# A transformer layer whose output projection goes from plain products to seven products per 2x2 split

## The chip, the cores and the metric

The kernel runs on one core of a Trainium2 chip. The engines named here are PE (TensorE, matmuls), DVE (VectorE), ACT (ScalarE), POOL (GpSimd) and SP (SyncE, which issues the DMA transfers). Each engine takes its instructions in the order of its own list and waits on semaphores for the others. The metric is the device time of one execution in microseconds (us).

## The reference, cut to what matters

One layer over 1024 tokens of width 1024: neighbourhood attention and retention, both from one input projection, merged by sigmoid gates, an output projection with a gated residual, a norm, and a gated convolutional MLP with a hidden width of 2816 (twice 22 blocks of 128).

```python
def _merge(o_na, o_ret, gate_na, gate_ret, w_proj_na, w_proj_ret, w_out):
    merged = jax.nn.sigmoid(gate_na) * (o_na @ w_proj_na) + jax.nn.sigmoid(gate_ret) * (o_ret @ w_proj_ret)
    return merged @ w_out
...
x = x + g1 * _merge(o_na, o_ret, xga, xgb, w_proj_na[l], w_proj_ret[l], w_out[l])
hx2 = _modulate(_rmsnorm(x, norm2_g[l]), sh2, sc2)
x = x + g2 * _conv_ffn(hx2, w_up[l], conv_w[l], conv_b[l], w_down[l])
...
def _conv_ffn(h, w_up, conv_w, conv_b, w_down):
    u = h @ w_up
...
    u = sum(up[:, i:i + n] * conv_w[i] for i in range(CONV_W)) + conv_b
    a, val = jnp.split(u, 2, axis=-1)
    return (jax.nn.silu(a) * val) @ w_down
```

## The kernel before, in words

Every float32 operand is split into a high and a low part in the matmul's own type (`split`: ACT casts the high part, DVE subtracts it to get the low one). A product is then three matmuls: high x high, high x low, low x high (`mm3`, `mm_a`, `open3`). A weight block reaches PE by `wload`: SP loads a raw tile of 128x512, ACT casts, DVE subtracts.

The stages, in order of time: input projection and neighbourhood attention (about 100 to 390 us of the span), retention (to 714), gates (768 to 921), the projection of the retention branch and the merge (`pret`, to 1008), output projection (to 1102), the MLP's up products (to 1540), the down projection (to 1752).

Large products are done in the manner of Strassen and Winograd: the two operands are cut in 2x2 and seven products of sums are made in place of eight. Class `Seven` does this for a unit of the gates and of the MLP's up product: it loads four weight blocks, POOL makes four sums s1 to s4 of them, and the steps 0 to 6 make the products A11 B11, S2 T2, S1 T1, S3 T3, A12 B21, A22 T4 and S4 B22. Here A stands for the weights and B for the activations; the T are differences of halves and quarters of the activations. The units are interleaved (`interleaved`), so that a unit's sums can be made in good time. The down projection uses the same seven products with the roles of the operands changed (table `DOWN`). Its weight sums are made beforehand: `down_sums` loads four blocks of w_down, has POOL subtract four times and stores the results in DRAM (`d_w`). Five of the eleven j are done in the retention, four in the gates (every third step), the last two beside `pret`.

In `pret` DVE multiplies a product by its gate, POOL adds the other branch, and the merged row block is split and kept (16 blocks, `mg`). The output projection is plain: `out_proj` makes, for each of 8 token blocks and 2 column halves, 8 x 3 matmuls. DVE multiplies by gate1 and adds x, ACT squares and sums, POOL takes the power, DVE scales: xn. `norm_out` transposes a token block (8 transposes of 128x128), ACT and DVE apply the modulation and split it, and for the second half of the tokens DVE makes the four T differences of that block and SP stores them to `d_t`. The MLP begins with two plain units (`up`, PLAIN = 2), in whose time `comb` loads and splits the T. `conv` follows each unit: ACT applies the middle tap from PSUM, DVE the two outer ones, ACT Silu, DVE the product; POOL makes sums for the down projection. From unit 2 on the units are `Up`, a `Seven`.

Order: the program's order is a start; when the kernel is built, a planner arranges each engine's list by estimated costs, SP's transfers among them. What is wrapped in `late` keeps its place in the program order on its engine. Pools of tiles with a fixed number of buffers set when a tile may be loaded again.

## Time and profile before

| | us |
|---|---|
| median of three runs | 1764.75 |
| the runs | 1764.75, 1764.78, 1760.84 |
| span of the profiled execution | 1759.2 |
| PE busy | 1726.0 (98%) |
| DVE busy | 1284.2 (73%) |
| ACT busy | 849.2 (48%) |
| POOL busy | 539.3 (31%) |

The profiled execution gives the span from its first to its last instruction; no run time of its own is listed beside it. In the views a stretch is given with its length, then for each engine its busy time and, in brackets, its number of instructions, and at the end PE's granted clock, the share of the DMA engines' time and GB/s. A group of instructions is given with line, engine, operation, output and inputs, its count, its busy time, the mean time of one in ns, and the idle time of the engine ahead of it with what ended that. A line of the timeline begins with the start and the duration in us; several instructions in a row are drawn together, with their count at the end. In a list of waits stand the total, the count and the longest.

### The profile page before, as it was taken

To read this page: it belongs to the slowest core of one execution; us is meant where nothing else is said; L and a number is where in the kernel's file an instruction comes from. 1 tells how busy PE (TensorE), PEld (TensorE's weight loads), DVE (VectorE), ACT (ScalarE), POOL (GpSimd) and SP (SyncE) were. 2 spreads that over 40 slices of the span, in tenths; PEclk is the share of its full clock that TensorE was granted. 3 is DMA by queue.
4 is the path that set the end of the run, shared out by engine and by line. 5 is a ranking of instruction groups with operands and counts; after the bars stand their busy time and mean duration, and the time that the engine had idled before them with its cause. 6 is when DMAs were issued, how large, how long until landed. Compare 5 with 4: busy or idle time off the path is not lost.

```text
span 1759.2 us, 24801 instructions
## 1 busy us (share of the span) xinstructions
PE 1726.0 (98%) x8405; PEld 1429.3 (81%) x8405; DVE 1284.2 (73%) x2454; ACT 849.2 (48%) x1826; POOL 539.3 (31%) x455
## 2 busy tenths in 40 slices
PE   8999999999999999999999999989999999999997
PEld 4688988888888888778888888778888888788886
DVE  4778887756776766777665557868899889875755
ACT  5666666653443434443444324534444444554444
POOL 1000000003334343555413300165555655211444
PEclk9999999999999999999999999999999999999999
DMA  9143334342231212677557733733322332586754
GB/s 348 61 130 125 95 117 147 117 133 87 73 108 43 72 42 68 203 238 239 200 199 268 246 143 132 254 108 102 108 90 92 118 120 90 170 296 192 239 162 162
DMA packets 139408, 261.10 MB, mean 148 GB/s; under 512 B 15856, under 2 KB 28304, under 8 KB 139280
## 3 DMA queue, kind: packets, MB, share of 16 engines
q1 hardware_dynamic: 139280, 259.51, 44.3%
q8 instruction: 66, 1.08, 0.3%
q14 instruction: 62, 0.51, 0.1%
HBM read 187.34 MB, written 69.48 MB: 146 GB/s over the span
## 4 chain that ended last, share of the span: by engine, by line
PE 43%; issue 6%; DVE 4%; POOL 3%; DMA 1%; ACT 1%; SPq 0%; POOLq 0%; ACTq 0%; DVEq 0%
PE u L1374 30%; PE y L1374 4%; PE pr L112 2%; PE pr L111 2%; PE pr L110 2%; PE om L122 1%; PE om L121 1%; PE om L123 1%; POOL x L1902 1%; DVE wc L87 0%; DVE b L1350 0%; DVE v L1679 0%; POOL pd L1939 0%; DVE hxT L87 0%; POOL x L1947 0%
## 5 line engine op out<-in xcount | busy, mean ns | idle before, releaser
L1374 PE MATMUL u<-T,wc 128*128 128x512 f32 x960 | 227.1, 392 | 5.1 <-ACT pu L1408 5.1
L1374 PEld LDWEIGHTS u<-T,wc 128*128 128x128 f32 x960 | 180.6, 189 | 45.7 <-ACT pu L1408 7.9
L1374 PE MATMUL y<-wc,ahl 128*128 128x512 f32 x924 | 210.6, 389 | 2.7 <-DVE wc L87 1.8
L1374 PEld LDWEIGHTS y<-wc,ahl 128*128 128x128 f32 x924 | 173.3, 188 | 39.7 <-DVE wc L87 2.5
L87 DVE TENSOR_TENSOR wc<-ur,wc 128x512 fp32r<-128x512 f32 x137 | 122.7, 897 | 65.8 <-ACT wc L86 65.8
L86 ACT CAST wc<-ur 128x512 fp32r<-128x512 f32 x137 | 85.0, 621 | 129.7 <-PE y L1374 72.3
L111 PE MATMUL mm<-low,wc 128*128 128x512 f32 (+1 forms) x328 | 124.0, 378 | 0.0
L1374 PE MATMUL u<-h2a,wc 128*128 128x512 f32 x480 | 112.3, 389 | 0.7 <-DVE pu L1417 0.7
L110 PE MATMUL mm<-hx,wc 128*128 128x512 f32 x264 | 107.4, 407 | 0.2 <-ACT wc L589 0.2
L1374 PEld LDWEIGHTS u<-h2a,wc 128*128 128x128 f32 x480 | 90.0, 188 | 19.8 <-DVE pu L1417 1.2
L112 PE MATMUL mm<-hx,wc 128*128 128x512 f32 x264 | 105.2, 399 | 0.0
L86 ACT CAST wc<-s 128x512 fp32r<-128x512 f32 x80 | 49.7, 623 | 93.2 <-PE u L1374 88.3
L123 PE MATMUL mm<-wc,low 128*128 128x512 f32 (+1 forms) x240 | 91.2, 380 | 0.0
L1374 PE MATMUL u<-hxT,wc 128*128 128x512 f32 x384 | 89.6, 389 | 0.0
L1508 POOL TENSOR_TENSOR col<-col,bcol 128x32 f32<-128x32 f32 x1 | 0.3, 253 | 280.7 <-DVE aw L538 280.7
L87 DVE TENSOR_TENSOR wc<-s,wc 128x512 fp32r<-128x512 f32 x80 | 83.5, 1046 | 3.8 <-ACT wc L86 3.4
L1374 PEld LDWEIGHTS u<-hxT,wc 128*128 128x128 f32 x384 | 72.1, 188 | 14.9
L87 DVE TENSOR_TENSOR wc<-raw,wc 128x512 fp32r<-128x512 f32 x92 | 68.0, 746 | 17.7 <-ACT wc L86 17.7
L121 PE MATMUL mm<-wc,hx 128*128 128x512 f32 x192 | 75.2, 392 | 0.6 <-ACT r L1105 0.6
L122 PE MATMUL mm<-wc,hx 128*128 128x512 f32 x192 | 75.2, 392 | 0.0
L1383 POOL TENSOR_TENSOR s<-ur 128x512 f32<-128x512 f32 x20 | 35.7, 1783 | 126.3 <-DVE wc L87 68.7
L86 ACT CAST wc<-raw 128x512 fp32r<-128x512 f32 x92 | 56.8, 621 | 33.0 <-PE pr L112 6.0
(393 smaller groups left out, 4671.3 us busy)
## 6 DMA issues: line engine op xcount, KB each, us to landing
ur<-in_w_up SPq DMA_DIRECT2D x80, 256.0 KB, 2.9
ur<-d_a SPq DMA_DIRECT2D x77, 256.0 KB, 3.1
aw<-in_w_ada SPq DMA_DIRECT2D x32, 512.0 KB, 3.3
pj<-in_w_down SPq DMA_DIRECT2D x44, 256.0 KB, 5.2
d_w<-pj SPq DMA_DIRECT2D x44, 256.0 KB, 2.0
d_a<-sa SPq DMA_DIRECT2D x44, 256.0 KB, 2.0
ur<-d_w SPq DMA_DIRECT2D x44, 256.0 KB, 3.8
d_a<-at SPq DMA_DIRECT2D x33, 256.0 KB, 2.7
```

The lines of the kernel that those rows point to most:

```text
L86: act.copy(hi, src)
L87: (lo_eng or vec).tensor_tensor(lo, src, hi.bitcast(F32), ALU.subtract)
L110: pe.matmul(out, wh, xh, start=k == 0, stop=False)
L111: pe.matmul(out, wh, xl, start=False, stop=False)
L112: pe.matmul(out, wl, xh, start=False, stop=k == n - 1)
L121: pe.matmul(out, ah, bh, start=first, stop=False)
L122: pe.matmul(out, ah, bl, start=False, stop=False)
L123: pe.matmul(out, al, bh, start=False, stop=last)
L1374: pe.matmul(out, a, b, start=first and n == 0, stop=last and n == 2, skip_group_check=True)
L1383: pool.tensor_tensor(self.s1, self.a21, self.a22, ALU.add)
L1508: pool.tensor_tensor(col[:, 16:48], col[:, 16:48], bcol[:, 16:48], ALU.add)
L1902: pool.tensor_tensor(z, z, fg[:, gs(dh)], ALU.mult)
```

## The change

- `out_sums` makes the four sums of w_out for each of four j during the attention: six loads of 256 KB (two blocks are loaded twice), four POOL subtractions and four stores to `d_wo`, with three buffers, driven by one `next(wsums)` per attention step. The sums of w_down that stood beside `pret` move to the gates, which now run them every second step.
- `pret` keeps the merged rows as they are, without splitting, in SBUF; `mg_sums` makes S1 to S4 of them on DVE.
- The output projection takes the seven products in the order of the down projection: for each product p and each j a pair of operands is loaded and split (`out_ops`), and four token blocks are multiplied (`out_steps`). Multiplication by gate1 and addition of x go to POOL (`gated`), but for the last product of each column half (`out_last`), with the small steps of the norm.
- The transposes go by k over four token blocks (`turn2`), mixed with the plain up products, which now run in four loops: unit 1 with half 1, unit 0 with half 1, unit 0 with half 0, unit 1 with half 0. POOL makes the T differences (`token_sums`).
- Units 2 and 3 make their two products without sums first (`head`: A11 B11 and A12 B21), ahead of the interleaved steps.
- The plain units' products are copied from PSUM by ACT before `conv`.

```diff
+    def out_sums():
+        def load(j, n):
+            t = na.tile([P, 512], F32, tag="os", bufs=3, name="os")
+            sync.dma_start(t, io["w_out"][n % 2, KH * (n // 2) + j])
+            return t
+
+        for j in range(KH):
+            b11, b12 = load(j, 0), load(j, 1)
+            yield
+            late(pool.tensor_tensor(b12, b12, b11, ALU.subtract))
+            b22 = load(j, 3)
+            yield
+            sync.dma_start(d_wo[j, 0], b12)
+            late(pool.tensor_tensor(b22, b22, b12, ALU.subtract))
...
+            sync.dma_start(d_wo[j, 2], y)
...
         if i == 0:
             ada_load()
+        if i > 2:
+            next(wsums, None)
...
-    RET_SUMS, GATE_SUMS = 5, 9
+    RET_SUMS = 5
...
-    gate_sums = down_sums(gr, RET_SUMS, GATE_SUMS)
+    gate_sums = down_sums(gr, RET_SUMS, NH)
...
-        if n % 3 == 1:
+        if n % 2:
             next(gate_sums, None)
...
+    ORDER = (("A11", "B11"), ("S2", "T2"), ("A12", "B21"), ("S3", "T3"), ("S1", "T1"), ("A22", "T4"), ("S4", "B22"))
...
-        h_, l_ = gtile(half, F32R, "mh"), gtile(half, F32R, "ml")
-        split(h_, l_, g)
-        mg[db, half] = (h_, l_)
...
+    def mg_sums(j):
+        for c, x, y, o, n in (("S1", "A21", "A22", ALU.add, 1), ("S2", "S1", "A11", ALU.subtract, 0), ("S3", "A11", "A21", ALU.subtract, 0), ("S4", "A12", "S2", ALU.subtract, 1)):
+            am[c, j] = gtile(n, F32, "s")
+            vec.tensor_tensor(am[c, j], am[x, j], am[y, j], o)
...
+    def out_ops(p, js):
+        tl = []
+        for j in js:
+            w = wload(out_source(j, ORDER[p][1]))
+            a = pair_tile("ahl")
+            split(a[:, 0], a[:, 1], am[ORDER[p][0], j])
+            tl.append((j, a, w))
+        return tl
...
+    def out_last(tb, dh, p, x):
+        z[tb, dh] = t = t_tile("z")
+        vec.tensor_tensor(t, bank(p % 2, tb % QB), gate1[:, cols(dh)], ALU.mult)
+        vec.tensor_tensor(t, t, x, ALU.add)
+        out_square(tb, dh)
+        s = ss[:, tb]
+        pool.tensor_scalar(s[:, 3:4], s[:, dh : dh + 1], 1.0 / D, s[:, 2:3], ALU.mult, ALU.add)
+        pool.tensor_tensor(s[:, 4:5], s[:, 3:4], mhalf[:, 0:1], ALU.pow)
...
+    def gated(t, tb, dh):
+        pool.tensor_tensor(t, t, gate1[:, cols(dh)], ALU.mult)
+        pool.tensor_tensor(t, t, x_rows(tb, dh), ALU.add)
...
+    def token_sums(k):
+        b11, b21, b12, b22 = v2[0, k], v2[0, k + KH], v2[1, k], v2[1, k + KH]
+        for c, o, x, y in ((0, b11, b12, b11), (2, b12, b22, b12), (1, b22, b22, b11), (3, b21, b21, b22)):
+            pool.tensor_tensor(o, x, y, ALU.subtract)
+            sync.dma_start(d_t[c, k], o)
...
+    out_steps(1, True, False)
+    for b in range(QB):
+        u2[b] = t_tile("u2")
+        vec.tensor_tensor(u2[b], bank(1, b), p1[b], ALU.add)
+    for b in range(QB):
+        gated(u2[b], b, 1)
...
+    for n in range(2):
+        for b in range(QB):
+            out_mm(6, b, t7[n : n + 1], False, True)
+    for b in range(QB):
+        turn2(1, KORD[b], bank(1, 2 + b % 2))
+        out_mm(6, b, t7[2:], False, True)
+        out_last(b, 1, 6, u2[b])
...
+    for n, k in enumerate(KORD):
+        turn2(0, k, bank(0, n % 2))
+        if k >= KH:
+            token_sums(k - KH)
+        for br in range(2):
+            up_k(us4[2 + br], wu[1][br], 1, k, n)
...
+        def head(self):
+            self.X, self.p1 = u_tile(), self.tmp()
+            self.prod(self.X, self.raw(self.src[0, 0]), "B11", True, False)
+            act.copy(self.p1, self.X)
+            self.prod(self.X, self.raw(self.src[0, 1]), "B21", False, True)
+            self.c11()
...
+    for n in range(PLAIN):
         for c in ((1, 0), (2, 3))[n]:
             combs[f"T{c + 1}"] = comb(c)
-        conv(j, *us2)
+        uu = [tap.tile([P, T], F32, tag="uu", bufs=4, name="uu") for _ in range(2)]
+        for br in range(2):
+            for half in range(2):
+                act.copy(uu[br][:, half * 512 : half * 512 + 512], us4[2 - 2 * n + br][half])
+        conv(seq[n], *uu)
     units = [Up(n, j) for n, j in enumerate(seq)]
+    for i in range(PLAIN, PLAIN + HEADS):
+        units[i].head()
     for i, n in interleaved(PLAIN, NF):
-        units[i].step(n)
+        if i >= PLAIN + HEADS or n not in (0, 4):
+            units[i].step(n)
```

More of the change, by code (lines that the diff above doesn't have):

```diff
@@ L1040, in tile_hybrid_layer @@
     for _ in pieces:
+        pass
+    for _ in wsums:
         pass
@@ L1617, in tile_hybrid_layer @@
             pret(db, half)
-            next(out_sums, None)
-    pjp.release()
-    wo = {}
-    for kb in range(KB):
-        t = wop.tile([P, 2, 512], F32R, tag="wo", bufs=KB, name="wo")
-        wo[kb, 0] = wload(io["w_out"][0, kb], into=t)
+        if db >= KH:
+            mg_sums(db - KH)
     hxpool.release()
@@ new lines, in out_mm, with out_steps, out_square @@
+    def out_mm(p, b, tl, first, last):
+        ts = slice(b * P, (b + 1) * P)
+        for j, a, w in tl:
+            open3(bank(p % 2, b), a[:, 0, ts], a[:, 1, ts], w[:, 0], w[:, 1], first and j == 0, last and j == KH - 1)
+    def out_steps(p, first, last, n=KH):
+        for j in range(n):
+            tl = out_ops(p, (j,))
+            for b in range(QB):
+                out_mm(p, b, tl, first, last)
+    z, xn, v2 = {}, {}, {}
+    def out_square(tb, dh):
+        junk = t_tile("junk")
+        act.activation(junk, z[tb, dh], AF.Square, accum_out=ss[:, tb, dh : dh + 1])
+        sync.dma_start(d_x1[tb * P : (tb + 1) * P, cols(dh)], z[tb, dh])
@@ new lines, in tile_hybrid_layer @@
+    out_steps(3, False, False)
+    for b in range(QB):
+        u3[b] = t_tile("u3")
+        vec.tensor_tensor(u3[b], bank(1, b), p1[b], ALU.add)
+    for b in range(QB):
+        gated(p1[b], QB + b, 0)
+    out_steps(4, True, False)
+    for b in range(QB):
+        z[QB + b, 1] = u3[b]
+        vec.tensor_tensor(u3[b], bank(0, b), u3[b], ALU.add)
+        gated(u3[b], QB + b, 1)
+        out_early(QB + b, 1)
+    out_steps(5, False, True, 2)
+    tl = out_ops(5, (2, 3))
+    t7 = out_ops(6, (0, 1))
@@ L1719, in tile_hybrid_layer @@
+    wu[0] = [up_load(seq[1], br) for br in range(2)]
+    for br in range(2):
+        for n in range(KB):
+            up_k(us4[br], wu[0][br], 0, n, n)
     op.release()
@@ L1780, in comb @@
     def comb(c):
-        t = [tpl.tile([P, 4, KH, P], F32R, name=f"T{c}{i}") for i in range(2)]
-        for b in range(4):
-            raw = ur_load(d_t[c, b])
-            split(t[0][:, b], t[1][:, b], raw.rearrange("p (k t) -> p k t", k=KH))
+        t = [tpl.tile([P, KH, 512], F32R, name=f"T{c}{i}") for i in range(2)]
+        for k in range(KH):
+            split(t[0][:, k], t[1][:, k], ur_load(d_t[c, k]))
         return t
@@ L1815, in dst @@
         def dst(self, b, half):
-            return self.u[b][:, half * 512 : half * 512 + 512]
+            return self.out(b)[:, half * 512 : half * 512 + 512]
         def c11(self):
```

246 lines of the change are left out of this document (127 added, 119 removed).

## The prediction

> **What bounds the kernel now.** I read the engines' shares first, then stretches of 44 us, then the waits of PE, SP's timeline, and the groups of POOL, DVE and ACT.
>
> ```profile
> span 1759.2 us, 24801 instructions
> PE 1726.0 (98%) x8405; PEld 1429.3 (81%) x8405; DVE 1284.2 (73%) x2454; ACT 849.2 (48%) x1826; POOL 539.3 (31%) x455
> ...
> PE u L1374 <- ACT pu L1408: 5.1, 1, 5.1
> ...
> 1052.00:1096.00 44.00, 44.00 (x211) 36.59 (x211) 30.77 (x82) 16.88 (x38) 2.19 (x4) 1.00 0.34 130
> 1140.00:1184.00 44.00, 38.85 (x165) 31.73 (x164) 30.61 (x36) 16.65 (x25) 30.14 (x18) 0.96 0.35 115
> 1188.00:1232.00 44.00, 44.00 (x195) 36.16 (x194) 39.44 (x41) 21.12 (x30) 22.21 (x13) 1.00 0.34 107
> ```
>
> PE is the bound nearly everywhere (98% busy; the third column of a stretch is its busy time). A full stretch holds 195 matmuls of 128x512, so one costs 44 / 195 = 0.2256 us; the longer time shown for a single one overlaps its neighbours. The stretch from 1052 holds 211, of which 32 are the 128x128 transposes L1671: (44 - 179 x 0.2256) / 32 = 0.113 us each. The one large hole inside is in the stretch from 1140: 30 matmuls are missing and the granted clock is 0.96. The wait behind it is the 5.1 us in PE's list. Hence two rules for what follows: a matmul removed is 0.2256 us won; and as PE has no slack after a wait, a new wait of PE is lost in full.
>
> The median of the runs is 1764.75 us, 5.5 us more than the profiled span. I take these 5.5 us as unchanged and apply the sum to both alike.
>
> **1. Fewer products.** Eight row blocks x 2 column halves x 8 k x 3 = 384 matmuls become 7 products x 4 blocks x 4 j x 3 = 336; transposes (64) and plain up products (192) keep their number. -48 x 0.2256 = **-10.8 us**.
>
> **2. The old wait before the first sum unit.** It is meant to be filled by the two heads (48 matmuls, 10.8 us).
>
> ```profile
> 1150.35 1.07 PE L1374 MATMUL u<-T,wc 128*128 128x512 f32 x4
> 1156.57 3.62 PE L1374 MATMUL u<-T,wc 128*128 128x512 f32 x8 [5.15 <-ACT pu L1408]
> ```
>
> PE stops at 1150.35 + 4 x 0.226 = 1151.3 and resumes at 1156.57: 5.3 us. The next eight take 3.62 us, where eight at full rate take 0.39 + 7 x 0.226 = 1.97: after a wait of this length about 1.65 us more go to the half-speed clock. Gone: **-6.9 us**. I add 1.7 us to each new wait of several us below.
>
> **3. Weight sums ahead of the attention.** In the changed program SP's list has, between the load of aw and the copy of kH0, ten loads of w_out, five stores to d_wo and the two raw loads that stood there before; each store waits for a POOL subtraction, and with three os buffers the fourth and later loads wait for a subtraction or for a store that has landed. SP takes its list in order, so kH0 waits behind all of them.
>
> ```profile
> 87.62 0.42 SPq L530 DMA_DIRECT2D aw<-in_w_ada  x1
> 93.08 4.94 SPq L91 DMA_DIRECT2D raw<-in_w_qkv  x2
> 98.15 1.17 SPq L409 DMA_DIRECT2D kH<-kH  x2
> ...
> raw<-in_w_qkv SPq DMA_DIRECT2D x1, 256.0 KB, 2.7
> ...
> kH<-kH SPq DMA_DIRECT2D x1, 320.0 KB, 4.1
> raw<-in_w_qkv SPq DMA_DIRECT2D x1, 256.0 KB, 3.2
> d_w<-pj SPq DMA_DIRECT2D x44, 256.0 KB, 2.0
> ...
> 102.28 0.39 PE L112 MATMUL mm<-hx,wc 128*128 128x512 f32 x1
> 102.51 0.28 PE L472 MATMUL sl<-kH,qS 128*128 128x256 f32 x1
> ...
> L1901 POOL TENSOR_SCALAR ssf<-ssf 128x1 f32<-128x1 f32 x8 | 3.2, 400 | 1.4 <-ACT xr L1897 0.8
> L1907 POOL TENSOR_TENSOR ssf<-ssf,mhalf 128x1 f32<-128x1 f32 x8 | 4.7, 586 | 0.5
> L1593 POOL TENSOR_TENSOR sg<-sg 128x512 f32<-128x512 f32 x14 | 19.9, 1421 | 86.9 <-DVE sg L1592 77.3 <-DMA raw<-in_w_pret 4.2 <-ACT wc L86 2.9
> L1939 POOL TENSOR_TENSOR pd<-pd,xr 128x512 f32<-128x512 f32 x4 | 6.8, 1740 | 0.0
> 1201.57 1.29 POOL L1384 TENSOR_TENSOR s<-s,ur 128x512 f32<-128x512 f32 x1 [3.14 <-issue]
> ```
>
> The copy starts at 98.15 and takes 4.1 us, so kH0 lands at 102.3 and PE, having issued its last product at 102.28, reads it at 102.51: no slack. The new list, with a load at 2.6, a subtraction at 1.3 (the solitary POOL row) plus 0.5 for its start, a store at 2.0, an issue at 0.4: loads from 88.0; first store issued 93.0 and landed 95.2; the second store 94.6; load of x 95.3; third store 98.0, landed 100.2; y loaded at 98.4, subtracted by 102.8; fourth store 103.0, landed 105.2; the next j's b12, asked for at 103.4, is subtracted by 107.8; its store 108.0; then a load, raw and kH0 at 109.2. That is 11.0 us after 98.15. PE's scores, in order, come 10.9 us later: with the clock **+12.6 us**. Bounds: 0 if the chain were run before 98; 18 if its loads take 3.2 and its subtractions 1.74 (L1939). I take the short times of the nearest rows, since little else is moving there. The later sums stand among the ada loads, and PE reads the next kH only after sixteen more score products: 0 (to 2).
>
> **4. Gates and pret.**
>
> ```profile
> L1249 POOL TENSOR_TENSOR pj<-pj 128x512 f32<-128x512 f32 x44 | 62.7, 1426 | 7.5 <-DMA pj<-in_w_down 7.0
> ```
>
> The subtractions for w_down in the gates rise from 16 to 24, 8 x 1.43 = 11 us more of POOL over some 150 us, with eight loads and stores more. In pret DVE gets 16 row sums and loses 16 splits of merged rows, ACT loses 16 casts. I allow **+1 us** (0 to 3) for one late sum.
>
> **5. The seven products.** S is their start; one lasts 48 x 0.2256 = 10.8 us. POOL now multiplies by gate1, adds x and makes the small ops of the norm, in this order: u2 8 ops, z 4 with a small one after each that waits for ACT's square, p1 8, u3 8 with 4 small, then two small ones for each out_last.
>
> ```profile
> 1201.96 1.45 DVE L87 TENSOR_TENSOR wc<-s,wc 128x512 fp32r<-128x512 f32 x1
> ...
> L1654 ACT ACTIVATE xn<-x 128x1024 f32<-128x1024 f32 x1 | 1.1, 1063 | 0.2 <-DVE x L1651 0.2
> L87 DVE TENSOR_TENSOR wc<-s,wc 128x512 fp32r<-128x512 f32 x20 | 19.9, 1002 | 3.5 <-ACT wc L86 3.4
> L87 DVE TENSOR_TENSOR wc<-raw,wc 128x512 fp32r<-128x512 f32 x6 | 4.1, 684 | 0.0
> ```
>
> A split that DVE begins at 1201.96, while POOL is busy from 1201.57 to 1202.86, takes 1.45 us where it takes 0.684 alone: it ends 0.55 after POOL's. So the two get in each other's way; here DVE makes two splits per step of 2.7 us beside POOL. POOL's price lies between 1.29 (alone) and 1.74 (L1939, with the same splits at the same pace); I take 1.6. u2 is there at S + 22.5: ends 35.3; z: 4 x (1.6 + 0.4 + 0.75 for a square of half L1654's size, an estimate from its 1.06 with the sum's read-out) = 11, 46.3; p1 12.8, 59.1; u3 12.8 + 1.6, 73.5; four pairs of 0.4 and 0.586, 77.4; scaling, 78. PE wants all four blocks of xn after product six and two steps of seven: 26 x 2.71 = S + 70.4. Wait 7.6, with the clock **+9.3 us**. Bounds: 1 at 1.29 (POOL then waits for product five), 13 at 1.74.
>
> On this the Trainium skill, "SBUF — State Buffer", section "SBUF: two separate sides", is stricter: a DVE operation with two SBUF inputs and a GpSimd operation that reads SBUF hold a shared pair of ports in turn, the other "fully blocks". The row agrees that the split waited; the pair above took 1.84 us where blocking alone would give 1.97. That every POOL op meets a split is the first rival.
>
> **6. Turns, plain ups, and the heads.** Loop 2 turns half 0 and has POOL make 16 token sums; loops 3 and 4 are products only. From its start L2, PE takes 32 x 0.113 + 144 x 0.2256 = 36.1 us to the end U of loop 4. In the changed program DVE's and ACT's lists after the turns are: T2, T1, conv of the first unit, T3, T4, conv of the second, and only then the heads' weights; the heads' banks also wait for ACT's copies of u. Before, conv read PSUM and the T were long there.
>
> ```profile
> d_t<-v SPq DMA_DIRECT2D x4, 256.0 KB, 2.0
> ur<-d_t SPq DMA_DIRECT2D x4, 256.0 KB, 3.2
> ...
> L86 ACT CAST T<-ur 128x512 fp32r<-128x512 f32 x16 | 8.9, 617 | 3.5 <-DMA d_t<-vo 3.3 <-DMA ur<-d_t 0.2
> L1762 ACT ACTIVATE ta<-ta 128x1024 f32<-128x1024 f32 x5 | 5.3, 1061 | 8.4 <-DVE ta L1761 8.4
> L1759 ACT ACTIVATE ta<-uu,cb,cw 128x1024 f32<-128x1024 f32 x3 | 3.7, 1245 | 1.7 <-DVE uu L1398 1.7
> L1408 ACT COPY pu<-u 128x512 f32<-128x512 f32 x5 | 2.9, 574 | 2.1 <-PE u L1374 2.1
> L1762 ACT ACT_TABLE_LOAD x1 | 1.3, 1283 | 0.0
> L87 DVE TENSOR_TENSOR T<-ur,T 128x512 fp32r<-128x512 f32 x16 | 10.2, 684 | 2.3 <-ACT T L86 2.3
> L1763 DVE TENSOR_TENSOR at<-ta,at 128x1024 f32<-128x1024 f32 x5 | 6.1, 1214 | 0.0
> L1760 DVE SCALAR_TENSOR_TENSOR ta<-uu,cw,ta 128x1023 f32<-128x1023 f32 x3 | 3.9, 1285 | 0.0
> ```
>
> POOL's first token sum can start after two turns of 1.8 us and DVE's pass, L2 + 5; six at 1.6 beside the turns, ten at 1.29: done at L2 + 27.5. SP issues the T loads behind all sixteen stores; the fourth goes out at 29.1 and lands 3.2 later: D = L2 + 32.3. From D, ACT: a cast, four T1 casts and four copies of u (4.8), ta (1.245): 6.7. DVE: four steps of conv, 5.1: 11.8; T3, 2.7: 14.5; its last sum, 1.2, after ACT's table load and Silu: 15.7; T4: 18.4. ACT meanwhile: at, T3, half T4 to 11.6, table and Silu to 14.0, rest of T4, four copies of u to 17.5, ta to 18.75. DVE's second conv 5.1: 23.9; the split of the first head weight 0.68: 24.6. The heads run from L2 + 56.9, PE is free at 36.1: 20.8, with the clock **+22.5 us**. Bounds: 16 with every token sum at 1.29, no table load and loops that DVE makes 3 us longer; 28 with every sum at 1.74. The heads are behind the very chain they should cover; what follows them is covered.
>
> In loop 1 DVE has four gate/add/scale groups beside four turns, but POOL's lateness in step 5 has let it catch up: 0 (to 3).
>
> **Sum.** -10.8 - 6.9 + 12.6 + 1 + 9.3 + 22.5 = +27.7: span 1786.9, time 1764.75 + 27.7 = **1792 us**.
>
> **Rivals.** (a) Full exclusion of POOL and DVE: each POOL op of step 5 costs 1.29 + 0.68 = 1.97 and xn is ready at S + 88: 17.6 + 1.7 instead of 9.3, and two more us on the token sums: 1804. For it: the split row; against: L1939's 1.74. Chance 0.12. (b) SP's chain is hidden, because the stores and loads of the sums overlap more than I let them: 1792 - 12.6 = 1779. For it: SP's raw load at 93.08 came 5 us after the ada load even without the sums. 0.12. (c) The chain from token sums to conv ends near U, the heads then do their work: 1792 - 22.5 = 1770. Against: 24.6 us of DVE and ACT work between D and the heads, each piece with its row. 0.1. (d) The other side: a waiting instruction doesn't hold what stands behind it. Then kH0 goes at 98, the heads' splits pass conv, and only steps 1, 2, 4 and 5 are left: 1764.75 - 17.7 + 1 + 9.3 = 1757, faster by 0.4%. It decides as soon as steps 3 and 6 together cost less than 7 us. Against it stand two rows:
>
> ```profile
> SPq L91 <- DVE wc L87: 14.9, 5, 5.0
> ...
> 1153.50 1.26 DVE L87 TENSOR_TENSOR wc<-ur,wc 128x512 fp32r<-128x512 f32 x1 [2.67 <-ACT wc L86]
> ```
>
> Between 84 and 106 us SP stands 14.9 us for raw buffers that DVE frees, and issues nothing meanwhile; in the old gap DVE stands 2.67 us for a cast. 0.1, a third of which ends as no change. That the heads simply don't fill the gap they are named for is my forecast, step 6.
>
> **Chances and range.** The forecast holds 0.56, with its own range 1784 to 1800. Going down to (c) and up to (a), 1769 to 1805 leaves out (d) and the far ends. About 0.3% (5 us) is what tells a change from none here. Faster 0.08, same 0.04, slower 0.88.
>
> **What would show it.** Step 1: 336 products in the out stage. Step 3: kH's copy issued near 109 instead of 98, PE idle some 11 us before its first scores. Step 5: PE waiting for xn before the first half-1 transposes, POOL ops of 1.5 to 1.75 us, no gap on POOL. Step 6: T's loads behind d_t's last store, PE idle some 20 us after the last plain up product, ended by a head's wc. Wrong would be: kH copied on time; POOL at 1.3 us; heads starting within 5 us of loop 4.

## The result, and the profile after

The changed kernel takes 1836.09 us (median of four runs, 1830.01 to 1839.51) against 1764.76 before: a ratio of 1.0401, 95% interval 1.0379 to 1.0424. The forecast was 1792 and its range ended at 1805. The direction came as forecast, the size did not: +71 us instead of +27.7.

The profiled execution took 1830.01 us, the fastest of the four, with a span of 1828.2; by spans the change costs 69.0 us. A run is thus some 1.8 us longer than its span. The 5.5 us that the prediction carried between span and median before were mostly the spread between runs, not a fixed cost.

First the head of the page of the kernel after, then its stretches of the output stage up to the first transpose of xn, of the rest up to the last plain up product, and of the 36 us behind that. The columns are those of the stretches shown before.

```profile
span 1828.2 us, 24941 instructions
PE 1736.2 (95%) x8357; PEld 1428.1 (78%) x8357; DVE 1322.5 (72%) x2378; ACT 860.8 (47%) x1842; POOL 635.7 (35%) x531
```

```profile
1028.84:1128.51 99.67, 78.72 (x314) 59.69 (x312) 68.19 (x82) 38.39 (x77) 46.43 (x40) 0.92 0.42 134
1128.51:1204.06 75.55, 65.27 (x280) 49.47 (x280) 50.16 (x68) 32.15 (x57) 28.93 (x28) 0.92 0.43 151
1204.06:1240.00 35.94, 18.40 (x60) 13.00 (x61) 33.73 (x27) 21.10 (x34) 22.37 (x12) 0.72 0.51 164
```

PE fell from 98% to 95% busy. In the first stretch no engine is full: PE 79 of 100 us, DVE 68, ACT 38, POOL 46. That is the picture of engines waiting for each other, not of one that has too much work. It is the main thing that the prediction missed: 312 products at 0.2256 us are 70.4 us, so 29.3 us are lost there.

Where the 69.0 us lie, by the start of each stage's first PE instruction in the two timelines:

| stage | before, us | after, us | difference | forecast |
|---|---|---|---|---|
| to the first scores | 102.5 | 115.1 | +12.6 | +10.9 (step 3) |
| attention | 300.2 | 305.0 | +4.8 | +1.7 (step 3, the slow clock behind the wait) |
| retention, transposes, gates | 518.1 | 519.2 | +1.1 | 0 |
| projection and merge | 87.0 | 89.5 | +2.4 | +1 (step 4) |
| output projection to the last plain up product | 140.0 | 175.2 | +35.3 | -1.5 (steps 1, 5, loop 1) |
| rest | 611.4 | 624.2 | +12.8 | +15.6 (steps 2, 6) |

**The start.** SP's timeline of the kernel after, and PE's wait there:

```profile
88.10 1.37 SPq L1011 DMA_DIRECT2D os<-in_w_out  x3
94.81 0.33 SPq L1020 DMA_DIRECT2D d_wo<-os  x1
...
110.29 1.17 SPq L409 DMA_DIRECT2D kH<-kH  x2
```

```profile
115.14 0.55 PE L472 MATMUL sl<-kH,qS 128*128 128x256 f32 x1 [10.99 <-DMA kH<-kH]
```

The copy of kH goes out at 110.29 (before: 98.15; forecast: 109.2), behind the stores to `d_wo`; PE stands 10.99 us, and the products after it run slow for a while (the next three start 0.35, 0.22 and 0.21 us apart, before 0.12).

**The seven products.** From the list of waits between 1028 and 1130 us, three of PE and two of ACT:

```profile
ACT wc L86 <- DMA raw<-d_wo: 25.3, 4, 11.0
...
ACT junk L1725 <- POOL u L1746: 10.0, 4, 3.8
...
PE u L1752 <- DVE z L1734: 7.6, 1, 7.6
PE u L1408 <- DVE ahl L87: 7.5, 5, 2.6
...
PE u L1408 <- ACT ahl L86: 5.6, 5, 2.0
```

Read from the bottom: PE waits ten times, 13.1 us together, for a split pair (`ahl`), and once, 7.6 us, ahead of the first transposes of xn. The other 8.6 of the 29.3 us lost are products at a slower pace (granted clock 0.92). ACT's casts of weights wait 25.3 us in four pieces for raw tiles. Why the tiles are late stands in SP's timeline:

```profile
1053.90 10.52 SPq L1688 DMA_DIRECT2D xr<-in_x  x4
1064.55 4.73 SPq L91 DMA_DIRECT2D raw<-d_wo  x4
...
1085.64 10.03 SPq L1688 DMA_DIRECT2D xr<-in_x  x4
...
1105.61 10.44 SPq L1726 DMA_DIRECT2D d_x<-u  x4
```

Three times SP needs 10 us for four transfers. The row tiles of x have four buffers, which come free with POOL's additions; the stores of x wait for those additions themselves. While POOL works through its eight operations, SP issues no weights. ACT has the same trouble: its squares (`junk`) wait 10.0 us for POOL, with casts behind them.

The groups of DVE and POOL from 1050 to 1122 us give the second part, and the timeline shows one burst:

```profile
L87 DVE TENSOR_TENSOR wc<-raw,wc 128x512 fp32r<-128x512 f32 x16 | 20.0, 1266 | 15.6 <-ACT wc L86 15.6
L1745 POOL TENSOR_TENSOR u<-u,gate 128x512 f32<-128x512 f32 x8 | 12.4, 1561 | 38.2 <-ACT wc L86 30.5 <-DVE u L1806 7.7
...
L87 DVE TENSOR_TENSOR ahl<-s,ahl 128x512 fp32r<-128x512 f32 x10 | 11.5, 1156 | 6.7 <-ACT ahl L86 6.7
...
L87 DVE TENSOR_TENSOR ahl<-sg,ahl 128x512 fp32r<-128x512 f32 x6 | 8.0, 1344 | 1.4 <-ACT ahl L86 1.4
```

```profile
1053.84 1.74 POOL L1745 TENSOR_TENSOR u<-u,gate 128x512 f32<-128x512 f32 x1
...
1054.35 1.78 DVE L87 TENSOR_TENSOR wc<-raw,wc 128x512 fp32r<-128x512 f32 x1
```

POOL's price, 1.49 to 1.59 us in the mean of a group, is close to the 1.6 that I took. But the price is paid by both: DVE's splits cost 1.16 to 1.34 us in the mean, up to twice the 0.684 of before, and in a burst the two engines go in step, some 1.7 us for a split beside a POOL operation.

The wait of 7.6 us is another matter. It is ended not by xn but by `z` L1734: the third block's product is read out of the PSUM bank that the first transposes are to write. On DVE this reading stands behind xn of the two blocks before it, and each xn waits for POOL's two small operations, which wait for ACT's square of that block. DVE's timeline, then POOL's:

```profile
1122.95 0.49 DVE L1741 TENSOR_SCALAR xn<-z,ss 128x512 f32<-128x512 f32 x1 [1.79 <-POOL ss L1739]
...
1127.37 0.49 DVE L1741 TENSOR_SCALAR xn<-z,ss 128x512 f32<-128x512 f32 x1 [0.80 <-POOL ss L1739]
1127.77 0.68 DVE L1734 TENSOR_TENSOR z<-u,gate 128x512 f32<-128x512 f32 x1
```

```profile
1114.41 1.29 POOL L1746 TENSOR_TENSOR u<-u,xr 128x512 f32<-128x512 f32 x1
...
1122.02 0.26 POOL L1738 TENSOR_SCALAR ss<-ss 128x1 f32<-128x1 f32 x1 [5.29 <-ACT junk L1725]
```

POOL had ended its last large operation at 1115.70, 5.2 us before PE ran out of products at 1120.91, and stood idle for 5.29 us before the first of those two small ones. So this wait is a chain from engine to engine, block by block, and not POOL's backlog.

**The end of the plain units.** PE, then DVE, in the kernel after:

```profile
1203.67 0.39 PE L123 MATMUL u<-h2a,wc 128*128 128x512 f32 x1
1217.61 2.26 PE L1408 MATMUL u<-h2a,wc 128*128 128x512 f32 x4 [13.55 <-ACT wc L86]
...
1225.59 6.58 PE L1408 MATMUL u<-h2a,wc 128*128 128x512 f32 x19 [3.38 <-DVE wc L87]
```

```profile
1196.59 0.69 DVE L87 TENSOR_TENSOR T<-ur,T 128x512 fp32r<-128x512 f32 x1 [11.79 <-ACT T L86]
...
1216.00 2.29 DVE L1888 SCALAR_TENSOR_TENSOR ta<-uu,cw,ta 128x1023 f32<-128x1023 f32 x1
...
1224.86 0.68 DVE L87 TENSOR_TENSOR wc<-ur,wc 128x512 fp32r<-128x512 f32 x1
```

The order is the one of step 6: T, conv of the first unit, T, conv of the second (from 1216.00), and then the split (1224.86) that the heads need. Four products of a head slip in at 1217, four of a T product at 1220.

### The profile page after: what moved, and what is told of

Same layout as the page of the kernel before. It is cut to its first block, busy times and chain, and to the rows that moved or that the text cites. A ratio compares the mean times of both kernels' runs of the same rounds, so it can differ in the third digit from the quotient of the medians.

```text
span 1828.2 us, 24941 instructions
## 1 busy us (share of the span) xinstructions
PE 1736.2 (95%) x8357; PEld 1428.1 (78%) x8357; DVE 1322.5 (72%) x2378; ACT 860.8 (47%) x1842; POOL 635.7 (35%) x531
## 5 line engine op out<-in xcount | busy, mean ns | idle before, releaser
L87 DVE TENSOR_TENSOR wc<-raw,wc 128x512 fp32r<-128x512 f32 x118 | 98.9, 847 | 64.7 <-ACT wc L86 62.1
L86 ACT CAST wc<-raw 128x512 fp32r<-128x512 f32 x118 | 73.0, 619 | 96.9 <-PE pr L112 38.0
L1408 PE MATMUL u<-wc,ahl 128*128 128x512 f32 x336 | 88.2, 419 | 13.3 <-DVE ahl L87 7.5
L1408 PEld LDWEIGHTS u<-wc,ahl 128*128 128x128 f32 x336 | 66.0, 201 | 33.2 <-DVE ahl L87 11.8
L121 PE MATMUL mm<-wc,hx 128*128 128x512 f32 x192 | 75.3, 392 | 0.6 <-ACT r L1140 0.6
```

Source lines behind the costliest of these rows:

```text
L86: act.copy(hi, src)
L87: (lo_eng or vec).tensor_tensor(lo, src, hi.bitcast(F32), ALU.subtract)
L121: pe.matmul(out, ah, bh, start=first, stop=False)
L1408: pe.matmul(out, a, b, start=first and n == 0, stop=last and n == 2, skip_group_check=True)
```

## The experiments

**One cause each.** Three runs take one suspected cause out of the changed kernel, a fourth leaves the heads out.

e1_pin wraps the loads and stores of `out_sums` in `late`, so that SP keeps them in the program's order:

```diff
-            sync.dma_start(t, io["w_out"][n % 2, KH * (n // 2) + j])
+            late(sync.dma_start(t, io["w_out"][n % 2, KH * (n // 2) + j]))
-            sync.dma_start(d_wo[j, 0], b12)
+            late(sync.dma_start(d_wo[j, 0], b12))
...
```

> Only the loads and stores of the weight sums in the attention keep their place in the program's order; SP then has raw, raw and the kH copies straight behind the ada load, as in the kernel before. If the wait at the attention's start is made by SP's list (step 3): kH's copy is issued near 98 instead of 110 us, PE's 11.0 us wait for kH is gone with its 1.7 us at half clock, and the attention behind it gets back its 300 us; time 1836 - 13 to -17 = 1819 to 1823. If the sums cost by their traffic and POOL work, wherever they stand: the wait at kH goes, but comes back later in the attention as waits of the ada loads or of d_ona; less than 5 us won.

It took 1815.91 us (1.0297 of before, 1.0279 to 1.0315), 20.2 less than the change by medians and 15.4 by spans. SP's timeline of this run:

```profile
93.12 4.95 SPq L91 DMA_DIRECT2D raw<-in_w_qkv  x2
98.19 1.17 SPq L409 DMA_DIRECT2D kH<-kH  x2
```

The copy is back at 98.19, the scores start at 102.66, and the attention falls from 305.0 to 301.2 us. So SP's list costs not only the 12.6 us ahead of the scores, but 3.8 more inside the attention, where 1.7 were worked out. The gain is above the 13 to 17 us expected.

e2_sp takes most of SP's waits for POOL away: ten buffers for x rows, and ACT issues the stores of x.

```diff
-        t = op.tile([P, 512], F32, tag="xr", bufs=4, name="xr")
+        t = op.tile([P, 512], F32, tag="xr", bufs=10, name="xr")
-        sync.dma_start(d_x1[tb * P : (tb + 1) * P, cols(dh)], z[tb, dh])
+        act.dma_start(d_x1[tb * P : (tb + 1) * P, cols(dh)], z[tb, dh])
```

> In the seven products of the output projection the buffers of x rows go from 4 to 10 and the stores of the new rows are issued by ACT, behind the square that waits for the same rows. SP's list then hardly waits for POOL; POOL's and DVE's work is the same. Theory A (the weights come late, because their loads stand on SP behind loads and stores that wait for POOL; 38 us of such waits on SP in the changed kernel): PE's losses of 28.6 us between the start of the projection and the first transpose fall to under 12; time 1836 - 16 to -25 = 1811 to 1820. Theory B (DVE is slow because each split waits for a POOL operation: 1.77 us instead of 0.68 in the bursts): the losses stay above 22; time 1830 or more. Splits stay slow in the bursts under both.

1822.44 us (1.0327, 1.0311 to 1.0342), 13.7 less; the stretch up to the first transpose falls from 99.7 to 90.2 us. The loss there falls from 29.3 to 19.8 us, between the two theories. SP's waits for POOL are 16.9 us where they were 47.1, so the test is not a clean one. PE now waits for ACT's casts in two pieces, and ACT for POOL.

```profile
PE u L1408 <- ACT ahl L86: 11.2, 2, 6.3
...
ACT junk L1725 <- POOL u L1746: 11.4, 4, 4.8
```

e5_sq adds to e2_sp that ACT's squares stand one product later in the program order (and keep that place), so that casts stand ahead of them.

```diff
-        act.activation(junk, z[tb, dh], AF.Square, accum_out=ss[:, tb, dh : dh + 1])
+        late(act.activation(junk, z[tb, dh], AF.Square, accum_out=ss[:, tb, dh : dh + 1]))
...
-        out_early(QB + b, 1)
...
+    for b in range(QB):
+        out_early(QB + b, 1)
...
```

> As e2_sp (more buffers for x rows, stores of the rows issued by ACT), and ACT's squares of z and u3 are asked for one product later, so that the casts of the next weights don't stand behind squares that wait for POOL. In e2_sp PE still lost 19 us ahead of the first transpose, its largest waits (6.3 and 5 us) ended by a cast of ACT. If ACT's list is what was left: losses under 10 us, time 8 to 12 us below e2_sp, 1811 to 1815. If the slow splits beside POOL's bursts are what was left: losses stay at 15 to 20 us, time 1818 to 1823.

1824.24 us (1.0334, 1.0313 to 1.0355), no gain on e2_sp; the stretch is 87.8 us, with 17.4 us lost. PE's waits for split pairs fell from 12.1 to 7.0 us, but its waits for z and xn at the first transposes rose from 3.0 to 7.9. The squares' place is not what was left.

e3_dve keeps SP's list and gives POOL's additions and multiplications by gate1 to DVE.

```diff
-        pool.tensor_tensor(t, t, gate1[:, cols(dh)], ALU.mult)
-        pool.tensor_tensor(t, t, x_rows(tb, dh), ALU.add)
+        vec.tensor_tensor(t, t, gate1[:, cols(dh)], ALU.mult)
+        vec.tensor_tensor(t, t, x_rows(tb, dh), ALU.add)
...
-        pool.tensor_tensor(z[b, 0], z[b, 0], x_rows(b, 0), ALU.add)
+        vec.tensor_tensor(z[b, 0], z[b, 0], x_rows(b, 0), ALU.add)
```

> gate1 and x are applied by DVE instead of POOL (28 operations of about 0.69 us more on DVE, 28 of 1.3 to 1.7 us fewer on POOL). Both theories lose their cause here, so this tells the size of the two together: the splits go back to 0.68 us, SP waits for DVE only briefly. Against it DVE has 19 us more to do. If DVE's own work does not become the bound: losses ahead of the first transpose under 10 us, xn ready earlier, time 1805 to 1815. If it does (about 75 us of work in the 76 us of products): no more than 8 us won, 1828.

1809.96 us (1.0251, 1.0236 to 1.0267), 26.1 less, the largest single gain. Up to the first transpose it takes 77.0 us for 324 products (73.1 at 0.2256), where the kernel after took 99.7 for 312 (70.4): 3.9 us lost instead of 29.3. DVE's groups of this run from 1040 to 1110 us:

```profile
L87 DVE TENSOR_TENSOR wc<-raw,wc 128x512 fp32r<-128x512 f32 x25 | 17.2, 686 | 0.7 <-ACT wc L86 0.7
...
L1745 DVE TENSOR_TENSOR u<-u,gate 128x512 f32<-128x512 f32 x8 | 5.1, 684 | 0.0
```

A split is at 0.686 us again, and the operation that takes POOL 1.56 takes DVE 0.684. The lists of SP and ACT are as they were; SP still stands, now for DVE's additions, up to 5.9 us at a time, but PE waits only 3.4 us in all up to 1110. So in this stage nearly all that was lost hangs on the work that POOL has there. Whether POOL's own price or the slow splits beside it weigh more, no run separates: e3_dve takes both away.

e4_h0 leaves the heads out:

```diff
-    PLAIN, HEADS = 2, 2
+    PLAIN, HEADS = 2, 0
```

> No heads: units 2 and 3 make their two products without sums in the interleaved order, as the units behind them. If the heads stand behind the second conv anyway (step 6) and cover nothing: PE waits as long after the last plain product, 18 to 25 us with its clock, and the time is 1836 within 6 us. If the heads do cover a part of the way to the sums: 5 to 10 us slower, 1841 to 1846.

1840.82 us (1.0432, 1.0417 to 1.0448), 4.7 more than the change; by stage, the rest behind the last plain product is 632.3 us instead of 624.2. So the heads seem to be worth some 5 to 8 us even where they come late; the two intervals overlap at their ends, and the time lies where the two theories meet.

**Together.** v0 is e1_pin and e3_dve in one.

> e1_pin and e3_dve together: weight sums in their place, gate1 and x on DVE. If the waits in the attention and in the projection are independent, the gains add: 1836 - 20 - 26 = 1790 (1786 to 1794). If the later wait eats a part of what the earlier one gives: 1795 to 1810.

1791.69 us (1.0148, 1.0131 to 1.0165): the two causes add.

v1 is v0 with the work around the heads moved: conv of the first plain unit ahead of loop 4, T1 and T2 behind the heads, the heads' weights through the raw buffers of the weight loads, and the banks and buffers that go with it.

```diff
+    uu = plain_out(0)
+    conv(seq[0], *uu)
+    wu[0] = [up_load(seq[1], br) for br in range(2)]
...
+    for i in range(PLAIN, PLAIN + HEADS):
+        units[i].head()
+    for c in (1, 0):
+        combs[f"T{c + 1}"] = comb(c)
...
-            self.prod(self.X, self.raw(self.src[0, 0]), "B11", True, False)
+            self.prod(self.X, rawload(self.src[0, 0]), "B11", True, False)
...
```

> v0, and the conv of the first plain unit is asked for ahead of the last loop of plain products, the heads' weights come through the stream's own buffers, free of the token sums' store, the heads' banks are those of the first unit, and the second conv comes after the sums of units 2 and 3. If step 6 is right (the heads wait for the chain from the token sums over T and two convs): PE's wait behind the last plain product falls from some 18 us to under 5, time 1790 - 15 to -20 = 1770 to 1775. If the wait is made by DVE's and ACT's total work there: it only moves behind the heads, less than 6 us won, 1784 or more.

1789.36 us (1.0137, 1.0122 to 1.0152). Only 2.3 less, as the second theory said: the wait moves. PE stands 6.4 us for a head's weight and 6.7 for copies, where v0 has 13.5 and 3.4 for weights. But the built order still has T splits ahead of conv, so that the chain of step 6 was not really taken away, and conv is slow:

```profile
1166.06 1.28 DVE L1885 SCALAR_TENSOR_TENSOR ta<-uu,cw,ta 128x1023 f32<-128x1023 f32 x1 [0.37 <-ACT ta L1884]
1167.26 2.32 DVE L1885 SCALAR_TENSOR_TENSOR at<-uu,cw,at 128x1023 f32<-128x1023 f32 x1
```

v2 is v1 with the token sums on DVE, behind loop 2; v3 is v2 with half 0's turns three steps later.

```diff
-            pool.tensor_tensor(o, x, y, ALU.subtract)
+            vec.tensor_tensor(o, x, y, ALU.subtract)
...
-        turn2(0, k, bank(0, n % 2))
+        if n >= LAG:
+            turn2(0, KORD[n - LAG], bank(0, n % 2))
...
```

> This is the version with conv of the first unit ahead of loop 4, changed in one thing: DVE makes the 16 token sums instead of POOL, and they stand behind loop 2 in the program order. Theory that POOL's token sums (bursts of 6.4 and 18.8 us, done at 1155) are what makes the T late and slows DVE's sums beside them: DVE makes 16 x 0.69 = 11 us of them in loops 3 and 4, where it has room; the T splits start some 10 us earlier, conv's outer taps take 1.28 us each again instead of 2.28, and the two waits of 6.6 and 5.2 us with their half clock go for the most part: 1773 to 1781. Rival that the total of DVE's and ACT's work between loop 2 and the end of the heads is the limit, whoever makes the sums: DVE gets 11 us more, the waits stay or grow: 1787 to 1795.

> As the run before it, and half 0's turns start three steps later (in the fourth step of loop 2), the last three stand in loop 3, token sums behind the first half of loop 3. Theory that xn simply comes a few us late for the turns (waits of 1 to 2 us each with their half clock, some 17 us in loops 1 and 2): PE does three steps of 1.35 us more before it asks for half 0's xn, the waits of loop 2 go and with them 4 to 8 us; the token sums end some 4 us later and cost nothing: 4 to 8 us under the run before it. Rival that DVE is full in loops 1 and 2 (11.4 to 11.9 us of 12): what PE does earlier it waits for later, and the T come later still: within 3 us of the run before it or slower.

1785.65 us (1.0119, 1.0104 to 1.0134) and 1783.24 us (1.0108, 1.0091 to 1.0124). In v2 conv is at 1.28 us again and the wait of 6.4 us for a head's weight is gone, but the waits for copies grow from 6.7 us to 11.0 (5.6 for ACT's and 5.4 for DVE's). By stage the gain lies ahead of the last plain product (148.2 us from the start of the output projection instead of 151.3), not behind it (624.4 instead of 623.0): between my two theories, 3.7 us of the 8 to 16 expected. v3 is 2.4 us lower, within the spread of four runs each and within the 3 us of its rival; in loop 1 the built order still mixes half 0's transposes in. What goes on there, DVE's timeline of v3 shows:

```profile
1108.85 0.49 DVE L1742 TENSOR_SCALAR xn<-z,ss 128x512 f32<-128x512 f32 x1 [1.79 <-POOL ss L1740]
1109.25 0.81 DVE L1759 TENSOR_SCALAR v<-u,a,col 128x512 f32<-128x512 f32 x1
1109.97 0.68 DVE L1735 TENSOR_TENSOR z<-u,gate 128x512 f32<-128x512 f32 x1
1110.57 0.68 DVE L1760 TENSOR_TENSOR h2l<-v,h2h 128x512 fp32r<-128x512 f32 x1
1111.17 0.69 DVE L1736 TENSOR_TENSOR z<-z,u 128x512 f32<-128x512 f32 x1
1113.64 0.48 DVE L1742 TENSOR_SCALAR xn<-z,ss 128x512 f32<-128x512 f32 x1 [1.79 <-POOL ss L1740]
```

From xn to xn it is 1113.64 - 1108.85 = 4.79 us, and DVE stands idle 1.79 of them. The norm of the next block begins with z, which stands behind xn and v of this one; then ACT squares, POOL makes two small operations, and xn follows. Here nobody is full; a latency runs round four engines, once per block.

v4 is v3 with this chain pipelined: on DVE z of the next block stands ahead of xn of this one (all `late`), and the transposes keep their order on PE.

```diff
-        vec.tensor_tensor(t, bank(p % 2, tb % QB), gate1[:, cols(dh)], ALU.mult)
-        vec.tensor_tensor(t, t, x, ALU.add)
+        late(vec.tensor_tensor(t, bank(p % 2, tb % QB), gate1[:, cols(dh)], ALU.mult))
+        late(vec.tensor_tensor(t, t, x, ALU.add))
...
         out_last(QB + b, 0, 5, p1[b])
+        out_pow(QB + b, 0)
+        if b:
+            out_scale(QB + b - 1)
...
```

> As the run before it (token sums on DVE, half 0's turns three steps later), and the norm's chain is pipelined: the multiplication by gate1 and the addition for block b+1 stand ahead of the scaling of block b on DVE, all four blocks of half 0 ahead of the turns' v where the program can, and the turns' transposes keep their place in the program order on PE. Theory that the waits of loop 1 (some 14 us with their half clock, in a cycle of 4.8 us per block: DVE's two z operations, ACT's square, POOL's two small operations, DVE's xn, PE's transposes, DVE's v, and only then the next z) come from one block's chain standing behind the other's in DVE's list and from transposes of half 0 that the planner puts between those of half 1: 7 to 13 us less than the run before it, 1770 to 1776, and the cycle gone from PE's list. Rival that DVE's and ACT's sum of work in loop 1 is the limit: 1780 to 1784, PE still waiting for xn or v once per block.

1778.17 us (1.0086, 1.0067 to 1.0104), 5.1 less; 7 to 13 were expected. PE's waits between 1088 and 1125 us, first in v3, then in v4:

```profile
PE u L1753 <- DVE xn L1742: 6.4, 5, 2.0
```

```profile
PE u L1758 <- DVE v L1764: 3.4, 2, 2.5
...
PE u L1758 <- DVE xn L1747: 0.6, 1, 0.6
```

The wait for xn fell from 6.4 to 0.6 us; one for v grew from 0.6 to 3.4 and takes part of it back. DVE is now busy 20.3 of the first 22 us behind the first transpose, so that the rival, DVE's sum of work, is near. v4 needs 141.5 us from the start of the output projection to the last plain product, where the kernel before takes 140.0 with 48 products more. It is the best version of the change that I ran, and still 0.9% slower than before.

**The old wait, in the kernel before.** The heads are to fill a wait of 5.3 us. In the trace of before the copy `pu<-u`, which ends it, stands on ACT behind a cast that waits 4.2 us for a load of w_up, and that load waits on SP for a free raw buffer. Three runs change this in the kernel before, with nothing of the change. br14 has two buffers more:

```diff
-rp.tile([P, 512], F32, tag="r", bufs=12, name="ur")
+rp.tile([P, 512], F32, tag="r", bufs=14, name="ur")
...
```

> The kernel before, with 14 instead of 12 buffers for the raw blocks and sums of the MLP's up product, and nothing of the change. It asks what the old wait ahead of the first sum unit (5.3 us and 1.65 of half clock, the one that the heads are to fill) hangs on. Theory that it is ACT's list: the copy pu<-u stands behind a cast that waits 4.2 us for a load of w_up, and SP issues that load at 1148 only because no raw buffer is free from 1140 on; with two more the load goes out some 7 us earlier, the wait shrinks by 3 us or more, and the time is 1757 to 1762 (0.2 to 0.4% under the kernel before). Rival that POOL's sums or ACT's own work between 1146 and 1156 hold the copy whatever the loads do: within 0.1% of the kernel before.

1773.67 us, slower than before (1.0047, 1.0033 to 1.0061). PE's wait did shrink to 2.6 us, but PE's waits from 1160 to 1540 us are these, in br14 and then in the kernel before:

```profile
PE u L1374 <- DVE pu L1417: 10.9, 9, 1.2
```

```profile
PE u L1374 <- DVE pu L1417: 0.7, 1, 0.7
```

With the two buffers the planner put a weight sum of the next unit between conv's sums on POOL. The unit's other sums follow at once and now run beside conv's outer taps, which makes DVE's `pu` late; each of nine rounds of units lost 1.2 us. An outer tap from 1170 to 1500 us, in br14 and then in the kernel before:

```profile
L1761 DVE SCALAR_TENSOR_TENSOR at<-uu,cw,at 128x1023 f32<-128x1023 f32 x17 | 37.3, 2194 | 0.6
```

```profile
L1761 DVE SCALAR_TENSOR_TENSOR at<-uu,cw,at 128x1023 f32<-128x1023 f32 x17 | 21.8, 1284 | 0.6
```

Neither the theory nor its rival had this. In bx1, next, the tap is at 1.284 us again and the nine waits are gone.

bx1 loads the one block that was late (A11 of unit 3) through the raw buffers of the weight loads:

```diff
+            if src is self.src[0, 0] and self.n == 3:
+                return rawload(src)
             return ur_load(src) if src is not None else rp.tile([P, 512], F32, tag="r", bufs=12, name="s")
```

> The kernel before, where the one block of w_up that ACT's list waited 4.2 us for (A11 of unit 3) is loaded into a raw buffer of the weight loads instead of one of the 12 of the up products; nothing else. In the built order this also sets the copy pu<-u and conv's outer taps ahead of that block's split, and leaves POOL's order of weight sums and conv's sums as it was (in the run before it that order had changed too). Theory that the old wait is the copy's place behind that cast, and that the run before it lost its gain again to POOL's changed order (1.4 us in each of nine rounds of units): the wait falls from 5.3 us to under 2 and nothing comes in its place: 1759 to 1762, 0.2 to 0.4% under the kernel before. Rival that DVE's and ACT's work after the last plain product is the limit, in whatever order: the wait stays above 3 us or moves to the next copies: within 0.1%.

1763.36 us, no difference (0.9997, 0.9988 to 1.0006). On ACT the copy is on time, and the cast behind it is not:

```profile
1151.41 0.59 ACT L1408 COPY pu<-u 128x512 f32<-128x512 f32 x1 [0.30 <-PE u L1374]
1163.44 0.62 ACT L86 CAST wc<-raw 128x512 fp32r<-128x512 f32 x1 [11.45 <-DMA raw<-in_w_up]
```

The wait moved to a later product of PE (4.5 us), as the rival said. bx3 loads the same block earlier, ahead of conv of the second plain unit:

```diff
+            if self.n == 3 and src is self.src[0, 0]:
+                return units3[0, 0]
...
+    units3 = {}
...
+        if n:
+            src = io["w_up"][seq[3], 0, 0]
+            units3[0, 0] = rawload(src)
         for c in ((1, 0), (2, 3))[n]:
```

> The kernel before, where A11 of unit 3 is loaded into a raw buffer of the weight loads ahead of the conv of the second plain unit, and cast from there; the order on ACT, DVE and POOL is that of the kernel before. In the run before this one the copy pu<-u was on time and the wait of 5.3 us gone, but the same load was late for the product after it (4.6 us). Theory that this one late load is all that the old wait hangs on: ACT's 4.2 us ahead of the cast go, the copy comes at about 1152.5 instead of 1155.9, PE waits 1 to 2 us instead of 5.3, and nothing comes in its place: 1759 to 1762. Rival that the next loads, sums or copies are just as late, so that the wait only moves again: 1763 to 1766.

1760.95 us (median of 12 runs): 0.9983 of before, 0.9973 to 0.9993.

```profile
1151.81 0.58 ACT L1408 COPY pu<-u 128x512 f32<-128x512 f32 x1
```

The copy comes at 1151.81 instead of 1155.93. PE's wait for it falls from 5.15 to 1.23 us, but with two more behind and ahead of it PE waits 2.9 us together; 1 to 2 were expected. So one late load made most of the wait at this place, and part of it came back nearby. From the last plain product to the last up product this trace takes 390.8 us, that of before 391.9: 1.1 us can be seen there. The median is 0.17% under the kernel before, but single runs spread over 1759.01 to 1765.81 here and came as low as 1759.31 in the kernel before, so how much of the 0.17% is this load stays open.

## Why the prediction was right or wrong

**Step 3 held.** The kH copy was forecast for 109.2 and came at 110.29, which refutes rival (b), that SP's chain is hidden; e1_pin gives the wait back. The first scores came 12.6 us later than before, where 10.9 were worked out: the other 1.7 of the step's 12.6 were for the slow clock, which falls behind the scores, so that the equal figure is partly chance. The attention then lost 4.8 us, 1.7 by the clock and "0 (to 2)" for the later sums; e1_pin returns 3.8 of them. The rest I did not take apart.

**Step 6 held in order and sum, with some luck.** The last plain product ended loop 4 at 1204.06 and the heads' bulk started at 1225.59: 21.5 us, where 20.8 were worked out. Two errors inside cancel. The second conv began on DVE 11.9 us after the last plain product, where the working has 15.0; and its four taps took 8.9 us instead of 5.1, at 2.28 to 2.30 each, beside POOL's weight sums. A few products at 1217 to 1222 came earlier, and the rest of the kernel lost 12.8 us instead of the 15.6 of steps 2 and 6. e4_h0 says that even late heads are probably better than none. That the chain of T and two convs alone makes the wait is not shown: v1, which was to take it away, got 2.3 us, and its built order kept T splits ahead of conv. Rival (c), that the heads cover, did not occur, and (d), that a waiting instruction holds nothing, is refuted by each of these traces.

**Step 5 failed, and not only in its size.** It has POOL's backlog make xn late, +9.3, and nothing else. The list shows a wait of 7.6 us at that place, the figure of the working before its clock term, but this is chance: POOL was done 5.2 us before PE asked, PE itself came to this point at S + 92.1 instead of S + 70.4, and the wait was made by the chain of z, square, power and xn, block by block. Output projection and plain units together lost 35.3 us, where steps 1 and 5 and loop 1 have -1.5. The failed piece is that POOL's lateness was followed along one path only. SP's x rows and stores and ACT's squares also wait for POOL, and the weights of the next products stand behind them: three stands of 10 us on SP, PE short of operands again and again from 1067 on. The step quoted the split that took 1.45 us beside POOL and costed POOL by it, but left DVE's splits at their price, which came to 1.16 to 1.34. "No gap on POOL" was wrong too: it idles 5 to 8 us several times, since its inputs are late in turn. e3_dve, which takes POOL out, leaves 3.9 of the 29.3 us lost in the first stretch; e2_sp, which takes 30 of SP's 47 us of waits for POOL out, leaves 19.8 (90.2 us for 312 products).

Rival (a), full exclusion of POOL and DVE, which stood beside the Trainium skill, "SBUF — State Buffer", section "SBUF: two separate sides", pointed to the right pair of engines. In the bursts a POOL operation and a split together took some 1.7 us, less than the 1.29 + 0.68 = 1.97 of strict turns and more than the 1.29 that the longer one takes alone: the section's turns fit these rows, but not for the whole recorded time of both. Its price of 1804 was still far from 1836, because it followed the same single path.

**Loop 1, "0 (to 3)", failed.** From the first transpose of xn to the last plain product the kernel after takes 75.6 us for 56.0 us of products and transposes (24 + 192 products of 0.2256, 64 transposes of 0.113); before, the whole output stage with these loops lost 3 us. Of the 19.6 us lost, 16.1 lie ahead of 1165.4, where loop 1 ends (72 products and 40 transposes). The argument was that DVE had caught up. It had, and it didn't matter: the chain z, square, power, xn, transposes, v ran in lockstep, 4.8 to 5.0 us per block (xn at 1143.31, 1148.32, 1153.11 and 1157.91; v3's rows show the same). v4, which pipelines it, gets 7.4 us back over both stretches, 5.1 in the median, and takes the loss behind the first transpose from v3's 18.2 to 12.8 us. What makes these 12.8 stays open.

**Steps 1, 2 and 4.** The products are fewer by 48; no run shows their 10.8 us alone, but v4's 141.5 us against 140.0 says that they are eaten where they were won. Step 2 counted on the old wait going with the heads; a larger one took its place. The projection lost 2.4 us (forecast 1, bound 3).

Left open: what remains of v4. Its span is 16.4 us over that of before (its median 14.2). By stage 6.3 lie behind the last plain product, around the heads, 3.9 in the projection, 1.6 in the output stage in place of 10.8 won, 2.5 in retention, transposes and gates, and about 1 each in the attention and ahead of it.

## What to carry to other kernels

When work moves to a slower engine, follow its lateness along every list that has an instruction waiting for it: transfers and casts queued behind such a wait stopped PE here with POOL busy for 46 of 100 us. Where a stretch shows no engine near full, look for a latency or a list: here the gains came from the place (e3_dve, e1_pin) and the order (v4) of operations, not from less work. A wait whose length matches the forecast proves little until the row says what ended it. And a change of buffers or of one load changes the built order elsewhere; compare the orders before reading the times.

## What the runs showed of the hardware that I had not expected

A 128x512 operation of POOL and a split of DVE slow each other both ways: 1.29 and 0.686 us alone, 1.49 to 1.59 and 1.16 to 1.34 in the mean of the output stage, where they meet in bursts. Conv's outer tap (128x1023) took 1.28 us with POOL at rest and 2.28 to 2.32 while POOL made sums. So moving POOL's gate and addition onto DVE, 28 operations at 0.684 or 19 us, cost DVE little more than the 18 us that its splits had lost beside POOL. After a wait of PE of 4.5 to 7.6 us the granted clock is 0.5 for a while and products come about 0.43 us apart instead of 0.2256: 3.3 us long in the kernel before (from 1156.57), 5.0 in bx1 (from 1164.11), 8.5 in the kernel after (from 1128.51, with shorter waits inside). In bx1 24 products after a wait of 4.5 us took 8.24 us where 24 took 5.60 in the kernel before.
